# Evacuations of PE's results placed three blocks behind PE instead of one, in the expert part of a two-layer kernel

## The chip, the cores and the metric

The kernel runs on one core of a Trainium2 chip. The metric is the device time of one execution in microseconds. The kernel before took 1711.92 us, the median of three runs between 1710.94 and 1712.4 us. The execution that was profiled took 1712.86 us, of which the profile's span covers 1711.2 us.

## The reference, cut to what matters

Two transformer-like layers run one after the other on 256 tokens of width 1024, in float32. The change touches the last part alone, a mixture of 64 experts in 8 groups of 8. A router picks one group for each token and the two best experts in it:

```
def expert_block(args):
    xb, e = args
    hid = jax.nn.silu(xb @ w_gate[e]) * (xb @ w_up[e])
    return hid @ w_down[e]
```

`w_gate[e]` and `w_up[e]` are 1024 x 512 and `w_down[e]` is 512 x 1024, so each expert brings 6 MB of weights for the few tokens that chose it. The result of an expert is weighted by the token's gate and added to the residual, and a root-mean-square norm ends the computation.

## The kernel before, in words

**Tiling.** The tokens of a group are gathered into one tile. All 64 experts are computed on the tile of their group. Products are formed in a reduced float format from parts: a weight tile is split into a rounded part `whi` (a cast on ACT) and the rest `wlo` (a subtraction on DVE, which reads `whi`), by `split` at L107. For a *small* group (at most 64 tokens) the token tile holds the rounded part in columns 0 to 63 and the rest in 64 to 127, and two matmuls, one with `whi` and one with `wlo`, do the work. Seven of the eight groups are small; the group with the most tokens takes a full tile and three matmuls.

**Blocks.** The work is a list of blocks `order`, numbered s. An expert has four blocks for gate (here G1 to G4), four for up (G5 to G8), and four for down (D0, D1, R, D2). A down stage comes after the gate and up stages of the *next* expert. A G block is four matmuls of 128x512 in a small group, as are D0, D1 and D2. R is the down block that uses its weights unsplit (L1379), so it asks nothing of ACT and DVE. An expert thus asks for 11 splits of 128x1024. After D2 of one expert PE turns the hidden values of the next one (`pht`, L1284), which that expert's down stage needs. The split tiles come from pools of six `whi` and six `wlo` buffers. The raw weights lie in a ring of 11 tiles of 1 MB each (`ring`), six loads to an expert, issued from SP in order as the tiles come free.

**Order.** From block 9 on the instructions of PE, ACT and DVE stand in exactly the order in which the Python loop writes them. At each block s the loop writes the splits of block s + 3 (`AHEAD` is 3), then PE's matmuls of block s, then one step of every generator in `steps`, and then `follow(s)`, which starts new generators. Each engine takes its own instructions in that order, and one that waits holds up all behind it.

**The generators.** `copied` takes a gate or up sum out of PSUM to `gu` (on ACT for a small group, L1396). `turned` takes `pht` through Silu (`hs`, ACT, L1287), the product with up (`hs`, DVE, L1289), the rounded part (`hidThi`, ACT, L1292) and the rest (`hidThi`, DVE, L1294). `prepare` gathers the tokens of the next group (`oh` on DVE, `pgx` on PE at L1228, `xghi`), once in a group. `summed` ends a group: it splits the down sums (`yghi` on ACT, `yglo` on DVE), multiplies them back to token order (`psct`, PE) and adds them to the residual (DVE, L291). A step that reads a result of PE was written in the block right after the one in which PE's matmuls stand.

A *visit* is a run of experts of one group: three experts of group 0, then groups 1, 2, 3, 7, 4, 5 and 6 with eight experts each, then the last five of group 0. Group 7 is the one with the full tile. A load of an expert that no token chose is skipped while its matmuls are not.

Of the kernel before, what the change touches and what calls it, by code (L numbers as in the profile page):

```python
# [32 lines left out]
def mega(ctx, tc, a, out, dbg=None):  # L33
# [256 lines left out]
    def add_res(t, n, ps):  # L290
        nc.vector.tensor_tensor(xres[:, t, cols(n)], xres[:, t, cols(n)], ps, op=OP.add)  # L291


    ps = acc.tile([P, 4, P], F32, tag="acc", name="warm")
# [69 lines left out]
    ps = acc.tile([P, 512], F32, tag="acc", name="bps")  # L364
# [5 lines left out]
    for t in range(NT):  # L370
# [12 lines left out]
        for q in range(2):  # L383
            ps = acc.tile([P, 4, P], F32, tag="acc", name="sps")
            for i in range(4):
                g = 4 * q + i
                nc.tensor.matmul(ps[:, i, :], wsT[:, g, :], vs[:, t, g * P:(g + 1) * P], start=True, stop=True)
            for i in range(4):
                g = 4 * q + i
# [25 lines left out]
    done = set()  # L415
# [159 lines left out]
    for t in range(NT):  # L575
        for n in range(2):
            sl = slice(n * 512, (n + 1) * 512)
            ps = mm.tile([P, 512], F32, tag="mm", name="ppj")
            for k in range(2):
                mm3(ps, pTs, wpp[k], (al, k, ts(t)), (al, sl), k == 0, k == 1)  # L580
            x = nc.vector.tensor_copy(prj[:, t, sl], ps)
# [124 lines left out]
    ps = mm.tile([P, 512], F32, tag="mm", name="cps")  # L706
# [509 lines left out]
    def prepare(keys, b, small, xgs, gws, v):  # L1216

        oh = mq.tile([P, NT, P], F32, name="oh", bufs=1)
        for t in range(NT):
            nc.vector.tensor_scalar(oh[:, t, :], slot2 if small else slot, keys[t], None, op0=OP.is_equal)  # L1220
        yield
        xg = [x[:, b] for x in xgb]
        w = GS if small else P
        kn = 512 // w
        pss = [acc.tile([P, kn, w], F32, tag="acc", name="pgx") for _ in range(KD // kn)]
        for t in range(NT):
            for k in range(KD):
                x = nc.tensor.matmul(pss[k // kn][:, k % kn, :], tA[:, t, k, :], oh[:, t, :w],  # L1228
                                     start=t == 0 and k % kn == 0, stop=t == 1 and k % kn == kn - 1)
                if t + k == 0 and ranked:  # L1230
                    fence(x, ranked.pop())
        yield
        for q, ps in enumerate(pss):
            ks = slice(kn * q, kn * q + kn)
            halves(two(xg[0]), ps) if small else split_ps(xg[0][:, ks, :], xg[1][:, ks, :], ps)
        xgs[v] = xg
        yield
        pgw = mm.tile([P, 512], F32, tag="mm", name="pgw")
        for t in range(NT):
            nc.tensor.matmul(pgw[:, :8], oh[:, t, :], wsel[:, t, :], start=t == 0, stop=t == 1)  # L1240
        ps = acc.tile([P, 4, P], F32, tag="acc", name="poh")
        for t in range(NT):
            nc.tensor.transpose(ps[:, t, :], oh[:, t, :], ident)
        yield
        gw = mq.tile([P, 8], F32, name="gw")
        nc.vector.tensor_copy(gw, pgw[:, :8])
        ohT = mq.tile([P, NT, P], F32R, name="ohT")
        nc.scalar.copy(ohT, ps[:, :NT, :])
        gws[v] = gw, ohT
        yield  # L1250
# [26 lines left out]
    def turned(hids, i, pp, gw, small, plain, hl=None):  # L1277

        hl = hl or hl_tile(mp, [P, 4, P], "hidT")
        if small:  # L1280
            ps = mm.tile([P, 2, 4, GS], F32, tag="mm", name="pht")
            for j, x in enumerate(pp):
                for q in range(4):
                    nc.tensor.matmul(ps[:, j, q, :], x[:, ts(q)], pairs, start=True, stop=True)  # L1284
            yield
            h = mp.tile([P, 4, GS], F32, tag="wr", name="hs")
            nc.scalar.activation(h, ps[:, 0], AF.Silu)  # L1287
            yield
            nc.vector.tensor_tensor(h, h, ps[:, 1], op=OP.mult)  # L1289
            yield  # L1290
            n = 3 if plain else 4
            nc.scalar.copy(two(hl[0])[:, :n, 0], h[:, :n])  # L1292
            yield
            nc.vector.tensor_tensor(two(hl[0])[:, :n, 1], h[:, :n], two(hl[0])[:, :n, 0].bitcast(F32), op=OP.subtract)  # L1294
            hids[i] = h, hl
        else:
            ps = mm.tile([P, 4, P], F32, tag="mm", name="pht")
            for q in range(4):
                nc.tensor.transpose(ps[:, q, :], pp[0][:, ts(q)], ident)
            yield  # L1300
            last_copy[0] = nc.scalar.copy(hl[0], ps)
            yield
            nc.vector.tensor_tensor(hl[1], ps, hl[0].bitcast(F32), op=OP.subtract)
            hids[i] = None, hl
        yield
# [6 lines left out]
    def summed(pd, ohT, done=lambda *x: None):  # L1312

        yg = (gp.tile([P, D], F32R, tag="xn", name="yghi"), gp.tile([P, D], F32R, tag="xn", name="yglo"))
        for n in range(2):
            split_ps(yg[0][:, cols(n)], yg[1][:, cols(n)], pd[n])
            yield
        for n in range(2):
            for t in range(NT):
                ps = acc.tile([P, 512], F32, tag="acc", name="psct")  # L1320
                for i in range(2):
                    nc.tensor.matmul(ps, ohT[:, t, :], yg[i][:, cols(n)], start=i == 0, stop=i == 1)
                yield
                add_res(t, n, ps)
                done(t, n, ps)

    AHEAD = 3

    def moe(keys, expert, visits, small=lambda g: False, skip=False, begin=(), on_the_way=iter(())):
# [59 lines left out]
        def copied(i, kind):  # L1389

            v, g, e, es = todo[i]
            gw = gws[v][0][:, e:e + 1]
            ps = sums.pop((i, kind))
            if small(g):
                x = mq.tile([P, F], F32, tag="hid", name="gu")
                nc.scalar.copy(x, ps) if kind == "g" else nc.scalar.mul(x, ps, gw)  # L1396
                gus.setdefault(i, []).append(x)
            elif kind == "g":
                x = mq.tile([P, F], F32, tag="hid", name="hid")
                nc.scalar.activation(x, ps, AF.Silu)  # L1400
                gus[i] = [x]
            else:
                nc.vector.scalar_tensor_tensor(gus[i][0], ps, gw, gus[i][0], op0=OP.mult, op1=OP.mult)
            yield

        def follow(s):

            i, kind, c = order[s]
            v, g, e, es = todo[i]
            last = s + 1 == len(order) or order[s + 1][:2] != (i, kind)  # L1410
            if kind in "gu":
                if last:
                    steps.append(copied(i, kind))
                if kind == "u" and last and e == es[max(0, len(es) - 4)] and v + 1 < len(visits):
                    g2 = visits[v + 1][0]
                    steps.append(prepare(keys(g2), (v + 1) % 2, small(g2), xgs, gws, v + 1))
                if i == 0 and kind == "u" and last:
                    finish(steps)
                    steps.append(turned(hids, 0, gus.pop(0), gws[v][0], small(g), plain(0)))
                return  # L1420
            if i + 1 < n and (last if i + 2 < n else c == 1):
                g1 = todo[i + 1][1]
                hl = [x[:, (todo[i + 1][0] + 1) % 2, :4] for x in xgb] if i + 2 == n else None
                x = turned(hids, i + 1, gus.pop(i + 1), None, small(g1), plain(i + 1), hl)
                next(x)
                steps.append(x)
            if last and e == es[-1] and i < n - 1:
                steps.append(summed(pds.pop(v), gws[v][1]))

        def finish(gens):  # L1430
            for x in gens:
                for _ in x:
                    pass
            gens.clear()
# [9 lines left out]
        with ExitStack() as fixed:  # L1444
            for s in range(len(order)):
                while ahead < len(order) and ahead <= s + AHEAD:
                    fetch(ahead)
                    ahead += 1
                if s == 4:
                    after.clear()  # L1450
                multiply(s)
                if s == 0:
                    with soon():
                        finish([prep])
                        for f in begin[2:]:
                            f()
                if skip and s == 8:
                    fixed.enter_context(tc.manual_schedule(engines={
                        mybir.EngineType.PE, mybir.EngineType.Activation, mybir.EngineType.DVE}))
                if s > 120:  # L1460
                    next(on_the_way, None)
                for x in list(steps):
                    if next(x, steps) is steps:
                        steps.remove(x)
                follow(s)
            finish(steps)
        with soon():
            finish([summed(pds.pop(len(visits) - 1), gws[len(visits) - 1][1], squares)])


    for i in range(9):
# [79 lines left out]
```

## Time and profile before

| | us |
|---|---|
| median of three runs | 1711.92 |
| profiled execution | 1712.86 |
| its span | 1711.2 |
| PE matmul busy | 1650.8 (96%) |
| PE weight load busy | 1287.7 (75%) |
| DVE busy | 1352.2 (79%) |
| ACT busy | 1136.8 (66%) |

The expert part takes the span from about 690 us on. A busy PE row counts overlapping matmuls whose ends are modelled, so the weight loads (PEld), which come one for each matmul, show PE's pace better. Idle time stands in brackets behind the instruction that followed it, with the engine and line whose result ended it. Where the engine named had long been done, something else ended the wait.

### The profile page before, as it was taken

How to read it: one execution, taken by the hardware profiler on the slowest of the kernel's cores; microseconds unless marked ns; L12 is line 12 of the kernel's file. 1: busy time of each engine (PE TensorE's matmuls, PEld its weight loads, DVE VectorE, ACT ScalarE, POOL GpSimd, SP SyncE). 2: the span in 40 equal slices, each digit the busy share in tenths (PEclk: the TensorE clock that was granted, in tenths of full speed). 3: DMA queues.
4: the chain of work that ended last, by engine and by line, in shares of the span. 5: the costliest groups of instructions: out<-in, count | busy, mean ns of one | idle time of the engine just before them, and what ended most of it. 6: DMA issues, size and time to landing. Idle time of an engine off the chain costs nothing. (4 is left out here: it accounts for less than half of the span.)

```text
span 1711.2 us, 24078 instructions
## 1 busy us (share of the span) xinstructions
PE 1650.8 (96%) x8474; PEld 1287.7 (75%) x8474; DVE 1352.2 (79%) x1643; ACT 1136.8 (66%) x1542; POOL 44.6 (3%) x69
## 2 busy tenths in 40 slices
PE   8999999999999998999999999999999999999996
PEld 7898789998898787666667666788776666666664
DVE  6665675556768866898998898898998898898996
ACT  5455454445566544877777877776877877877884
POOL 1000010000100310000000000000000000000000
PEclk9999999999999997999999999999999999999998
DMA  9953455554743284996996999998999999999961
GB/s 316 260 173 124 164 176 197 188 181 158 201 148 101 109 313 163 402 398 244 374 395 243 404 398 377 407 373 332 369 386 385 407 398 381 416 398 378 412 248 38
DMA packets 124882, 493.52 MB, mean 288 GB/s; under 512 B 9150, under 2 KB 53538, under 8 KB 78161
## 3 DMA queue, kind: packets, MB, share of 16 engines
q1 hardware_dynamic: 120160, 484.47, 75.2%
q0 software_dynamic: 1952, 6.05, 1.2%
q10 hardware_dynamic: 2640, 1.38, 0.3%
q8 instruction: 68, 1.11, 0.3%
q14 instruction: 62, 0.50, 0.1%
HBM read 509.30 MB, written 1.44 MB: 298 GB/s over the span
## 5 line engine op out<-in xcount | busy, mean ns | idle before, releaser
L107 DVE TENSOR_TENSOR wlo<-ring,whi 128x1024 fp32r<-128x1024 f32 x714 | 836.6, 1221 | 106.3 <-ACT whi L107 105.4
L107 ACT CAST whi<-ring 128x1024 fp32r<-128x1024 f32 x714 | 704.5, 1048 | 15.2 <-PE pgu L1274 5.8
L1275 PE MATMUL pgu<-wlo,xghi 128*128 128x512 f32 x896 | 363.4, 406 | 11.1 <-DVE wlo L107 11.1
L1274 PE MATMUL pgu<-whi,xghi 128*128 128x512 f32 x896 | 357.1, 399 | 1.4 <-DVE xghi L1211 1.4
L107 DVE TENSOR_TENSOR wlo<-raw,whi 128x1024 fp32r<-128x1024 f32 x173 | 211.9, 1233 | 137.1 <-ACT whi L107 135.7
L107 ACT CAST whi<-raw 128x1024 fp32r<-128x1024 f32 x173 | 180.2, 1048 | 188.9 <-PE pb L115 81.0
L1275 PEld LDWEIGHTS pgu<-wlo,xghi 128*128 128x128 f32 x896 | 169.3, 189 | 78.7 <-DVE wlo L107 48.1
L1274 PEld LDWEIGHTS pgu<-whi,xghi 128*128 128x128 f32 x896 | 169.6, 189 | 31.8 <-DVE xghi L1211 1.6
L1275 PE MATMUL pd<-wlo,hidThi 128*128 128x512 f32 x332 | 142.1, 428 | 8.4 <-DVE wlo L107 8.4
L114 PE MATMUL pb<-hThi,whi 128*128 128x256 f32 x480 | 137.5, 286 | 0.2 <-ACT hThi L129 0.2
L1274 PE MATMUL pd<-whi,hidThi 128*128 128x512 f32 x332 | 136.8, 412 | 0.0
L115 PE MATMUL pb<-hTlo,whi 128*128 128x256 f32 x480 | 135.8, 283 | 0.5 <-DVE hTlo L130 0.5
L116 PE MATMUL pb<-hThi,wlo 128*128 128x256 f32 x480 | 135.8, 283 | 0.0
L1284 PEld LDWEIGHTS pht<-pairs,gu 128*128 128x128 f32 x896 | 108.2, 192 | 4.3
L1284 PE MATMUL pht<-pairs,gu 128*128 128x64 f32 x896 | 106.0, 271 | 0.0
L1275 PEld LDWEIGHTS pd<-wlo,hidThi 128*128 128x128 f32 x332 | 62.3, 188 | 57.0 <-DVE wlo L107 49.5
L1379 PE MATMUL pd<-ring,hs 128*64 128x512 f32 x216 | 104.2, 605 | 0.0
L1287 ACT ACTIVATE hs<-pht 128x256 f32<-128x256 f32 x56 | 21.5, 383 | 120.9 <-PE pht L1284 120.8
L1274 PEld LDWEIGHTS pd<-whi,hidThi 128*128 128x128 f32 x332 | 62.4, 188 | 51.4 <-ACT whi L107 43.0
L115 PEld LDWEIGHTS pb<-hTlo,whi 128*128 128x128 f32 x480 | 91.9, 191 | 1.4 <-DVE hTlo L130 0.7
L114 PEld LDWEIGHTS pb<-hThi,whi 128*128 128x128 f32 x480 | 91.9, 191 | 1.2 <-ACT hThi L129 0.5
L116 PEld LDWEIGHTS pb<-hThi,wlo 128*128 128x128 f32 x480 | 91.9, 191 | 0.0
(430 smaller groups left out, 2350.7 us busy)
## 6 DMA issues: line engine op xcount, KB each, us to landing
ring<-in_w_gate_dram SPq DMA_DIRECT2D x128, 1024.0 KB, 7.3
ring<-in_w_up_dram SPq DMA_DIRECT2D x128, 1024.0 KB, 7.2
ring<-in_w_down_dram SPq DMA_DIRECT2D x126, 1024.0 KB, 7.5
raw<-in_w_in_dram SPq DMA_DIRECT2D x38, 1024.0 KB, 5.3
raw<-in_w_ff_dram SPq DMA_DIRECT2D x32, 1024.0 KB, 5.1
raw<-in_w_out_dram SPq DMA_DIRECT2D x12, 1024.0 KB, 4.9
raw<-in_w_in_dram SPq DMA_DIRECT2D x9, 512.0 KB, 4.6
raw<-in_w_ple_gate_dram SPq DMA_DIRECT2D x4, 1024.0 KB, 5.1
```

Of the source, the lines that this page charges most:

```text
L107: both = [nc.scalar.copy(hi, raw), nc.vector.tensor_tensor(lo, raw, hi.bitcast(F32), op=OP.subtract)]
L114: nc.tensor.matmul(ps, l[0][lsel], r[0][rsel], start=first, stop=False)
L115: nc.tensor.matmul(ps, l[0][lsel], r[1][rsel], start=False, stop=False)
L116: nc.tensor.matmul(ps, l[1][lsel], r[0][rsel], start=False, stop=last)
L1274: nc.tensor.matmul(ps, x[0][:, k, :], w[0][wsel], start=first, stop=False)
L1275: nc.tensor.matmul(ps, x[0][:, k, :], w[1][wsel], start=False, stop=last)
L1284: nc.tensor.matmul(ps[:, j, q, :], x[:, ts(q)], pairs, start=True, stop=True)
L1287: nc.scalar.activation(h, ps[:, 0], AF.Silu)
L1379: nc.tensor.matmul(pds[v][m][:GS, :], h[:, 3, :], wt[:, 0, cols(m)], start=False, stop=False)
```

## The change

Every generator step that reads a result of PE is written three blocks behind PE's matmuls instead of one. A step now returns how many blocks to wait before the next one (nothing stands for one), and `steps` holds that count beside the generator. The residual additions of `summed` also come one `psct` later: the addition of one is written after the matmuls of the next. At the next-to-last expert all open generators are finished before its turn is started.

```
-        yield
+        yield AHEAD            # behind pgx, poh/pgw, both forms of pht
...
     def summed(pd, ohT, done=lambda *x: None):
+        wait = []
+        yield AHEAD - 1
...
-                yield
-                add_res(t, n, ps)
-                done(t, n, ps)
+                yield 2
+                if wait:
+                    wait.pop()()
+                wait.append(lambda t=t, n=n, ps=ps: (add_res(t, n, ps), done(t, n, ps)))
+        yield 2
+        wait.pop()()
...
         def copied(i, kind):
             v, g, e, es = todo[i]
+            yield AHEAD - 1
...
                 x = turned(hids, i + 1, gus.pop(i + 1), None, small(g1), plain(i + 1), hl)
-                next(x)
-                steps.append(x)
+                steps.append([next(x), x])
...
                 for x in list(steps):
-                    if next(x, steps) is steps:
-                        steps.remove(x)
+                    x[0] -= 1
+                    if x[0] == 0:
+                        r = next(x[1], steps)
+                        if r is steps:
+                            steps.remove(x)
+                        else:
+                            x[0] = r or 1
```

The first place is ACT around the Silu of one expert of a small group. `pht_7415` is the turned hidden values, and the six `whi` tiles with `ring_6035` to `ring_6037` belong to G1 to G6, the blocks that PE takes right behind `pht_7415`. Before:

```order
L1396 ACTIVATE gu_7384<-pgu_7347,gw_6260 128x512
L107 CAST whi_7390<-ring_6035 128x1024
L107 CAST whi_7398<-ring_6035 128x1024
L107 CAST whi_7405<-ring_6036 128x1024
L107 CAST whi_7424<-ring_6036 128x1024
L1287 ACTIVATE hs_7433<-pht_7415 128x256
L107 CAST whi_7436<-ring_6037 128x1024
L107 CAST whi_7445<-ring_6037 128x1024
L1292 CAST hidThi_7413<-hs_7433 128x3x64
```

The same place on ACT now:

```order
L107 CAST whi_7388<-ring_6035 128x1024
L107 CAST whi_7396<-ring_6035 128x1024
L1402 ACTIVATE gu_7402<-pgu_7345,gw_6260 128x512
L107 CAST whi_7405<-ring_6036 128x1024
L107 CAST whi_7424<-ring_6036 128x1024
L107 CAST whi_7434<-ring_6037 128x1024
L107 CAST whi_7442<-ring_6037 128x1024
L1287 ACTIVATE hs_7450<-pht_7415 128x256
L107 CAST whi_7453<-ring_6038 128x1024
L107 CAST whi_7462<-ring_6038 128x1024
L1292 CAST hidThi_7413<-hs_7450 128x3x64
```

The copy of the up sum, the Silu and the rounded hidden values each stand behind two more casts: the Silu behind the casts of G1 to G6 instead of G1 to G4.

The second place is DVE where a group of tokens ends. `yglo` is the rest of its down sums, `psct` the sums in token order, `xres` the residual. Before:

```order
L130 TENSOR_TENSOR yglo<-pd,yghi 128x512
L107 TENSOR_TENSOR wlo<-ring,whi 128x1024 x2
L1294 TENSOR_TENSOR hidThi<-hs,hidThi 128x3x64
L291 TENSOR_TENSOR xres<-xres,psct 128x512
L107 TENSOR_TENSOR wlo<-ring,whi 128x1024
L291 TENSOR_TENSOR xres<-xres,psct 128x512
L107 TENSOR_TENSOR wlo<-ring,whi 128x1024
L291 TENSOR_TENSOR xres<-xres,psct 128x512
```

The same place on DVE now:

```order
L130 TENSOR_TENSOR yglo<-pd,yghi 128x512
L107 TENSOR_TENSOR wlo<-ring,whi 128x1024 x2
L1294 TENSOR_TENSOR hidThi<-hs,hidThi 128x3x64
L107 TENSOR_TENSOR wlo<-ring,whi 128x1024 x2
L291 TENSOR_TENSOR xres<-xres,psct 128x512
L107 TENSOR_TENSOR wlo<-ring,whi 128x1024 x2
L291 TENSOR_TENSOR xres<-xres,psct 128x512
L107 TENSOR_TENSOR wlo<-ring,whi 128x1024 x2
```

The four additions are spread over eight blocks instead of four. The order of the loads on SP is the same in both kernels.

## Rows read from the trace of the kernel before

**Rows 1.** Page, part 1: busy us (share of the span) x instructions.

```profile
PE 1650.8 (96%) x8474; PEld 1287.7 (75%) x8474; DVE 1352.2 (79%) x1643; ACT 1136.8 (66%) x1542; POOL 44.6 (3%) x69
```

**Rows 2.** Waits, 700 to 1690 us: us in total, times, longest.

```profile
ACT hs L1287 <- PE pht L1284: 117.9, 53, 3.7
DVE wlo L107 <- ACT whi L107: 94.4, 117, 2.7
PEld pd L1275 <- DVE wlo L107: 47.7, 104, 1.0
PEld pgu L1275 <- DVE wlo L107: 46.9, 105, 0.9
PEld pd L1274 <- ACT whi L107: 42.2, 52, 0.8
...
PE pgu L1275 <- DVE wlo L107: 10.9, 49, 0.5
PE pd L1275 <- DVE wlo L107: 8.1, 15, 0.6
...
PEld pgx L1228 <- DVE oh L1220: 4.8, 6, 0.8
...
DVE wlo L107 <- DMA ring<-in_w_up_dram: 0.5, 2, 0.3
```

**Rows 3.** Weight loads, one ordinary expert: start us, us, instruction [idle before <-releaser].

```profile
1536.81 0.19 PEld L1275 LDWEIGHTS pgu<-wlo,xghi 128*128 128x128 f32 x1
1537.04 0.19 PEld L1274 LDWEIGHTS pgu<-whi,xghi 128*128 128x128 f32 x1
1537.50 0.19 PEld L1275 LDWEIGHTS pgu<-wlo,xghi 128*128 128x128 f32 x1 [0.27 <-DVE wlo L107]
1537.60 0.19 PEld L1274 LDWEIGHTS pgu<-whi,xghi 128*128 128x128 f32 x1
...
1538.90 0.19 PEld L1275 LDWEIGHTS pgu<-wlo,xghi 128*128 128x128 f32 x1 [0.64 <-DVE wlo L107]
...
1539.47 0.19 PEld L1274 LDWEIGHTS pd<-whi,hidThi 128*128 128x128 f32 x1
1540.04 0.19 PEld L1275 LDWEIGHTS pd<-wlo,hidThi 128*128 128x128 f32 x1 [0.37 <-DVE wlo L107]
...
1541.17 0.19 PEld L1275 LDWEIGHTS pd<-wlo,hidThi 128*128 128x128 f32 x1 [0.37 <-DVE wlo L107]
```

**Rows 4.** ACT, the same expert.

```profile
1531.93 0.38 ACT L1287 ACTIVATE hs<-pht 128x256 f32<-128x256 f32 x1 [2.06 <-PE pht L1284]
...
1546.88 0.38 ACT L1287 ACTIVATE hs<-pht 128x256 f32<-128x256 f32 x1 [2.07 <-PE pht L1284]
```

**Rows 5.** DVE, the same expert.

```profile
1533.29 1.22 DVE L107 TENSOR_TENSOR wlo<-ring,whi 128x1024 fp32r<-128x1024 f32 x1 [1.45 <-ACT whi L107]
...
1536.22 1.23 DVE L107 TENSOR_TENSOR wlo<-ring,whi 128x1024 fp32r<-128x1024 f32 x1 [0.24 <-ACT whi L107]
1537.36 0.35 DVE L1294 TENSOR_TENSOR hidThi<-hs,hidThi 128x192 fp32r<-128x192 f32 x1
```

**Rows 6.** ACT's Silu at the ends of a visit and of a gathering expert.

```profile
1499.48 0.38 ACT L1287 ACTIVATE hs<-pht 128x256 f32<-128x256 f32 x1 [2.06 <-PE pht L1284]
...
1516.98 0.38 ACT L1287 ACTIVATE hs<-pht 128x256 f32<-128x256 f32 x1 [3.72 <-PE pht L1284]
...
1566.61 0.38 ACT L1287 ACTIVATE hs<-pht 128x256 f32<-128x256 f32 x1 [1.36 <-PE pht L1284]
```

**Rows 7.** Groups by line, 700 to 1690 us: busy, mean ns | idle before.

```profile
L291 DVE TENSOR_TENSOR xres<-xres,psct 128x512 f32<-128x512 f32 x32 | 21.8, 683 | 0.0
L130 DVE TENSOR_TENSOR yglo<-pd,yghi 128x512 fp32r<-128x512 f32 x16 | 11.0, 688 | 7.4 <-ACT yghi L129 7.4
```

**Rows 8.** A window while the ring first fills; last columns: DMA share, GB/s.

```profile
635.00:640.00 5.00, 4.42 (x38) 4.12 (x38) 4.22 (x9) 3.22 (x7) 0.56 (x1) 1.00 1.02 424
```

**Rows 9.** Page, part 6: loads of gate weights, KB, median us from issue to landing.

```profile
ring<-in_w_gate_dram SPq DMA_DIRECT2D x128, 1024.0 KB, 7.3
```

More of the change, by code (lines that the diff above doesn't have):

```diff
@@ L1243, in prepare @@
             nc.tensor.transpose(ps[:, t, :], oh[:, t, :], ident)
-        yield
+        yield AHEAD
         gw = mq.tile([P, 8], F32, name="gw")
@@ L1284, in turned @@
                     nc.tensor.matmul(ps[:, j, q, :], x[:, ts(q)], pairs, start=True, stop=True)
-            yield
+            yield AHEAD
             h = mp.tile([P, 4, GS], F32, tag="wr", name="hs")
@@ L1299, in turned @@
                 nc.tensor.transpose(ps[:, q, :], pp[0][:, ts(q)], ident)
-            yield
+            yield AHEAD
             last_copy[0] = nc.scalar.copy(hl[0], ps)
@@ L1322, in summed @@
                     nc.tensor.matmul(ps, ohT[:, t, :], yg[i][:, cols(n)], start=i == 0, stop=i == 1)
-                yield
-                add_res(t, n, ps)
-                done(t, n, ps)
+                yield 2
[4 more added lines that the diff above has]
+        wait.pop()()
     AHEAD = 3
@@ L1412, in follow @@
                 if last:
-                    steps.append(copied(i, kind))
+                    steps.append([1, copied(i, kind)])
                 if kind == "u" and last and e == es[max(0, len(es) - 4)] and v + 1 < len(visits):
                     g2 = visits[v + 1][0]
-                    steps.append(prepare(keys(g2), (v + 1) % 2, small(g2), xgs, gws, v + 1))
+                    steps.append([1, prepare(keys(g2), (v + 1) % 2, small(g2), xgs, gws, v + 1)])
                 if i == 0 and kind == "u" and last:
                     finish(steps)
-                    steps.append(turned(hids, 0, gus.pop(0), gws[v][0], small(g), plain(0)))
+                    steps.append([1, turned(hids, 0, gus.pop(0), gws[v][0], small(g), plain(0))])
                 return
@@ L1422, in follow @@
                 g1 = todo[i + 1][1]
-                hl = [x[:, (todo[i + 1][0] + 1) % 2, :4] for x in xgb] if i + 2 == n else None
+                hl = None
+                if i + 2 == n:
+                    finish(steps)
+                    hl = [x[:, (todo[i + 1][0] + 1) % 2, :4] for x in xgb]
                 x = turned(hids, i + 1, gus.pop(i + 1), None, small(g1), plain(i + 1), hl)
-                next(x)
-                steps.append(x)
+                steps.append([next(x), x])
             if last and e == es[-1] and i < n - 1:
-                steps.append(summed(pds.pop(v), gws[v][1]))
+                steps.append([1, summed(pds.pop(v), gws[v][1])])
         def finish(gens):
-            for x in gens:
+            for _, x in gens:
                 for _ in x:
@@ L1453, in moe @@
                     with soon():
-                        finish([prep])
+                        finish([[0, prep]])
                         for f in begin[2:]:
@@ L1467, in moe @@
         with soon():
-            finish([summed(pds.pop(len(visits) - 1), gws[len(visits) - 1][1], squares)])
+            finish([[0, summed(pds.pop(len(visits) - 1), gws[len(visits) - 1][1], squares)]])
     for i in range(9):
```

## The prediction

> **What bounds the kernel now.** I read the page's busy times first, then the list of waits over the expert part, then one ordinary expert in order of time on PE, ACT and DVE, and last the loads.
>
> The busy times name PE as nearly full, with 96%, but its weight loads are busy for only 75% of the span, and DVE and ACT for 79% and 66% [rows 1]. So nothing says yet that an engine is at its limit. The list of waits shows a circle. ACT's Silu waits for PE's `pht` 53 times, 117.9 us in all; DVE's splits wait for ACT's casts, 94.4 us; and PE's weight loads wait for DVE's `wlo` 209 times, 47.7 + 46.9 = 94.6 us [rows 2]. DVE waits for a load of weights for 0.5 us only [rows 2], so the data lie ready.
>
> The reader can see the circle in one expert. Silu starts come every 14.95 us (1531.93 to 1546.88). Before each, ACT stands idle for 2.06 us, because the Silu needs `pht` and the casts of G5 and G6 stand behind it [rows 4]. DVE has then nothing to subtract from, idles 1.45 us until G5's cast is done, and 0.24 us more later [rows 5]. It now runs behind PE, and PE pays at four loads, with 0.27, 0.64, 0.37 and 0.37 us idle [rows 3].
>
> What do these cost PE? An undisturbed load follows the one before by 0.23 us (1536.81, 1537.04). The waiting one came 0.46 us after its forerunner and the next only 0.10 us after it: 0.56 us for a pair that takes 0.46 [rows 3]. So of an idle time about 0.17 us is not lost. The four cost 1.65 - 4 x 0.17 = about 1.0 us, and PE alone would need 14.95 - 1.0 = 13.95 us for an ordinary expert. DVE alone would need 14.95 - 1.45 - 0.24 = 13.26 us [rows 4, 5]. Over the whole stretch PE loses 94.6 - 209 x 0.17 = 59 us. This is the most that the change can give, with 6 x (0.8 - 0.17) = 4 us for `pgx` behind `oh` [rows 2]: 63 us.
>
> The waits of 42.2 us in 52 pieces for `whi` at `pd` I don't count. Mean and longest are both 0.8 us [rows 2]; a wait for a varying supplier isn't that even. They come right behind the unsplit products of R, and I take them for PE's own time. If I am wrong there, up to 52 x 0.64 = 33 us more could come back.
>
> **A reading of the page that would give another sum.** PE's own matmul row shows idle time of only 10.9 + 8.1 us before `wlo` [rows 2]; by that row the change can give about 19 us, and the time would be 1694. The Trainium skill (Perfetto Trace Analysis, Identifying the Most-Contended Engine) says that the busy share of matmuls is no good measure, since pipelined instructions overlap, and that the busy share of the weight loads is to be used. The loads' 94.6 us are what I use, for the reason shown at the pair of loads.
>
> **The change, part by part.** It adds no instruction and takes none away; the order of the loads on SP stays.
>
> *Ordinary experts.* In the order of ACT the Silu now stands behind the casts of G1 to G6, no longer G1 to G4. ACT had 2.06 us of idle time there [rows 4], room for two casts, and DVE can split G5 and G6 while it would have waited. So when PE starts on G1, DVE has up to two splits of 1.22 us [rows 5] less before it: 2.4 us, where PE's loss shows that 1.0 was lacking. The lead need not be won in one expert; DVE needs 13.26 us for what takes PE 13.95, so it gains 0.7 us in each. The six buffers bound it: the cast of G6 takes the buffer that the last down block D2 gives back, and D2 stands before `pht`, so ACT can have that cast done while `pht` runs. What is late next is PE itself. With 53 Silus of small groups, 8 group ends (32 additions, four each) and 6 gathering experts [rows 2, 7], some 39 experts are ordinary: 39 x 1.0 = 39 us.
>
> *Queues that the steps are moved past.* The copy of the up sum to `gu`, which `pht` needs, stands behind two more casts on ACT. PE takes the four down blocks in between (about a third of the expert, over 4 us), two casts and a copy on ACT are under 3 us, so I cost it at nothing as long as the weights lie ready; if they don't, PE waits for a load two blocks earlier than before. The rest of the hidden values (`hidThi` on DVE) stands behind two more splits: that is a rival below. No DMA is issued by a moved step, and SP waits for the same releases in the same order.
>
> *Gathering experts.* Their period is 1566.61 - 1546.88 = 19.73 us [rows 4, 6]. The four waits of an ordinary expert go (1.0) and that for `oh` (0.6), which stands behind the same splits of DVE: 6 x 1.6 = 10 us. The new place of `xghi` behind `pgx` hides under the three blocks that now lie between.
>
> *Group ends.* Their period is 1516.98 - 1499.48 = 17.5 us [rows 6]. What is left of the 59 us belongs here and to the edges of the full-tile group: 59 - 39 - 6 = 14 us. Here DVE has four additions of 0.68 us and two `yglo` of 0.69 more than usual, 4.1 us [rows 7], PE eight matmuls of 0.23, 1.8 us. DVE then needs 17.4 us for what takes PE 15.8, 1.6 us too many. Its lead covers about 1. Bounds: all 14 us come back, or none. I take 14 - 8 x 0.6 = 9 us.
>
> *The end.* At the last expert the Silu, the product and the parts are written together, and the last additions one after the other; between nothing and 3 us more, I take 1.
>
> Sum: 39 + 10 + 9 - 1 = 57 us off the profiled execution's 1712.86: 1656. The median of the runs shown lies 0.9 us below that execution, so 1655.
>
> **Rivals.**
>
> *The loads become the bound.* Six loads of 1 MB are 6.29 MB for an expert; in 14.95 us that is 421 GB/s. While the ring first fills, with no consumer, the loads come at 424 GB/s [rows 8], so an expert in 13.95 us asks for 451, which was never seen. The Trainium skill (HBM Reference, Specifications (TRN2)) gives about 425 GB/s for a core that streams alone, bounded by its 16 DMA engines; by that page an ordinary expert would take an estimated 14.8 us and the gain there would nearly vanish. The trace's 424 agrees with the page. Against the rival stands that the loads are ahead: a tile of the ring is used ten tiles after the load is issued, 10 x 14.95 / 6 = 24.9 us, and the load lands after 7.3 [rows 9]: 17.6 us of lead. At 424 GB/s an expert's loads take 14.84 us, 118.7 for a visit of eight; PE would take 6 x 13.95 + (17.5 - 1.1) + (19.73 - 1.6) = 118.2. A visit so costs 0.5 us of the lead, and three visits in a row don't use it up. If nevertheless the loads hold every ordinary expert at 14.95, only gathering experts and group ends gain, 10 + 9 us, and perhaps the lead of 17.6 once: 1675 to 1693, middle 1684.
>
> *Half of the lead is lost.* The six buffers, or ACT's own work between casts, could let DVE come only one split further instead of two, or the next wait take over, as the product `hs` on DVE for which ACT's rounded part waits. Then about half of the 57 us comes back: 1683.
>
> *No lead at all.* If the buffers already held ACT at G4 before, the moved Silu changes nothing: 1712. Against it speaks that the cast of G5 came right behind the Silu and not at a release by PE.
>
> *Slower: the hidden values come too late.* The rest `hidThi` on DVE stood behind the split of G7 and now stands behind that of D0. Before it ended at 1537.36 + 0.35 = 1537.71, 1.76 us before PE's first load of D0 at 1539.47 [rows 3, 5]. Two more splits are 2.44 us. If DVE gets no earlier in time, it is 0.7 us late at D0 in each expert, on top of the waits of now: 53 x 0.7 = 37 us, 1749. The point that decides is whether DVE is at least 0.7 us earlier than before when it takes up G5. The idle 1.45 us before G5 [rows 5] speaks against it.
>
> **How the numbers follow.** My forecast holds 0.74, with 1646 to 1667 as its own range: all 63 us and a few of the waits at `whi`, or 46. The loads as the bound have 0.11, half of the lead 0.08, no lead 0.03, slower 0.03; 0.01 is for more than all the waits. The range of 8 in 10 takes in the forecast and most of the first two rivals: 1645 to 1686. About 0.2% (3.4 us) is what a measurement of this kernel tells from no change. Faster: 0.94; the same: 0.03; slower: 0.03.
>
> **What would show it.** Right: ordinary experts with Silus 13.9 to 14.1 us apart, PE's waits for `wlo` from 94.6 to under 25 us, DVE's wait for `whi` under 50, and periods near 16.4 at group ends and 18.1 at gathering experts. If ordinary experts stay at 14.9 and DVE's or ACT's waits name the ring, the loads are the bound. If PE's loads wait for `hidThi` at D0, the last rival is at work. If the matmuls' cadence of 0.23 us itself changes, or waits for `whi` at `pd` shrink, my floor for PE was wrong.

## The result, and the profile after

| | before | after |
|---|---|---|
| median | 1712.16 us (1710.94 to 1715.5, four runs) | 1650.59 us (1646.12 to 1652.82, four runs) |
| profiled execution, its span | 1712.86, 1711.2 us | 1649.3, 1647.6 us |

The ratio is 0.9634, with an interval of 0.9609 to 0.966: 61.6 us less between the medians, 63.6 between the profiled executions. 57 were forecast, with 63 as the most that could come. Medians and ratios in this document are of executions at a mean granted clock of 0.93 or more; one of the four of five splits ahead (below) ran at 0.552, took 2673.68 us and is left out of its figures.

The page's busy times after, each with its share of the span and its instructions, answer to [rows 1]:

```profile
PE 1607.0 (98%) x8474; PEld 1303.9 (79%) x8474; DVE 1353.2 (82%) x1643; ACT 1147.2 (70%) x1542; POOL 44.7 (3%) x69
```

The instructions are as many as before, and DVE is busy for as long as before, ACT for 10 us longer. What went is idle time. PE's matmul row counts 44 us less than before for the same 8474 matmuls, so part of what that row counted as busy was waiting. The waits of the expert part after (who waited for what: us in all, times, longest) answer to [rows 2]:

```profile
DVE wlo L107 <- ACT whi L107: 50.2, 111, 1.5
...
PEld pd L1274 <- ACT whi L107: 34.9, 43, 0.8
ACT hs L1287 <- PE pht L1284: 33.1, 50, 0.9
...
PEld pgu L1275 <- DVE wlo L107: 3.5, 6, 0.9
PEld pd L1384 <- DMA ring<-in_w_gate_dram: 3.3, 9, 0.4
PEld psct L1324 <- DVE xres L291: 3.2, 4, 0.8
PEld psct L1324 <- DVE wlo L107: 2.4, 3, 0.8
...
ACT whi L107 <- DMA ring<-in_w_down_dram: 1.0, 3, 0.3
ACT whi L107 <- DMA ring<-in_w_gate_dram: 0.9, 3, 0.3
```

The circle has come apart in the order in which it was closed: the Silu's wait for `pht` from 117.9 us to 33.1, DVE's for the casts from 94.4 to 50.2, and the weight loads' for `wlo` from 94.6 to 5.9. Of these only the 3.5 at gate and up are waits for `wlo`: the 2.4 at `psct` belong to the row of `pd` for `whi`, which still has 0.8 us a piece. In both kernels 53 loads of this stretch come right behind R, and each of them has 0.81 us of idle time before it. Before, all 53 were loads of `pd`. Now 46 are, three of them put down to `gu`, and seven are loads of `psct`, put down to `xres` or `wlo`.

One ordinary expert shows it in order of time. First ACT (start, duration, engine, line, operation; in brackets the idle time before it and what ended it), as in [rows 4]:

```profile
1540.29 0.38 ACT L1287 ACTIVATE hs<-pht 128x256 f32<-128x256 f32 x1 [0.57 <-PE pht L1284]
1541.04 2.00 ACT L107 CAST whi<-ring 128x1024 fp32r<-128x1024 f32 x2 [0.36 <-PE pgu L1274]
...
1554.22 0.38 ACT L1287 ACTIVATE hs<-pht 128x256 f32<-128x256 f32 x1 [0.56 <-PE pht L1284]
```

The Silus are 13.93 us apart (before 14.95), and ACT stands idle before one for 0.57 us instead of 2.06. Behind the Silu its next cast waits 0.36 us for a matmul of G1, whose buffers it takes over. Then DVE in the same expert, as in [rows 5]:

```profile
1542.12 1.23 DVE L107 TENSOR_TENSOR wlo<-ring,whi 128x1024 fp32r<-128x1024 f32 x1 [0.43 <-ACT whi L107]
...
1546.19 0.35 DVE L1294 TENSOR_TENSOR hidThi<-hs,hidThi 128x192 fp32r<-128x192 f32 x1
```

And PE's weight loads there, as in [rows 3]:

```profile
1546.31 0.19 PEld L1274 LDWEIGHTS pgu<-whi,xghi 128*128 128x128 f32 x1
1546.53 0.19 PEld L1275 LDWEIGHTS pgu<-wlo,xghi 128*128 128x128 f32 x1
...
1547.21 0.19 PEld L1274 LDWEIGHTS pd<-whi,hidThi 128*128 128x128 f32 x1
...
1551.26 0.19 PEld L1274 LDWEIGHTS pd<-whi,hidThi 128*128 128x128 f32 x1 [0.81 <-ACT whi L107]
```

No load waits for `wlo`; the cadence is 0.23 us, as before. The rest of the hidden values ends at 1546.54 on DVE, and D0's first load starts at 1547.21: 0.67 us to spare, where it was 1.76. In the expert part PE's matmuls waited for `hidThi` once, 0.8 us at 831 us. The Silus of a group end and of a gathering expert answer to [rows 6]:

```profile
1450.59 0.38 ACT L1287 ACTIVATE hs<-pht 128x256 f32<-128x256 f32 x1 [0.46 <-PE pht L1284]
1466.44 0.38 ACT L1287 ACTIVATE hs<-pht 128x256 f32<-128x256 f32 x1 [0.92 <-PE pht L1284]
...
1494.31 0.38 ACT L1287 ACTIVATE hs<-pht 128x256 f32<-128x256 f32 x1 [0.57 <-PE pht L1284]
1511.76 0.39 ACT L1287 ACTIVATE hs<-pht 128x256 f32<-128x256 f32 x1 [0.91 <-PE pht L1284]
1526.36 0.38 ACT L1287 ACTIVATE hs<-pht 128x256 f32<-128x256 f32 x1 [0.92 <-PE pht L1284]
```

A group end takes 15.85 us (before 17.5), a gathering expert 17.45 (before 19.73). The expert after a gathering one takes 14.60, not 13.93, since PE's work on `poh` and `pgw` has moved past the next `pht`. So the two together are to be compared: 32.05 us against 19.73 + 14.95 = 34.68.

Last the loads, in one window (busy time of PE, PEld, DVE, ACT, POOL, then granted clock, DMA share, GB/s), and the row of the gate loads in the list of issues, the answer to [rows 9]:

```profile
1300.00:1350.00 50.00, 50.00 (x232) 36.96 (x231) 48.67 (x50) 43.27 (x55) 0.00 (x0) 1.00 1.01 421
```

```profile
ring<-in_w_gate_dram SPq DMA_DIRECT2D x128, 1024.0 KB, 10.0
```

From 1300 to 1550 us the loads run at 420 to 421 GB/s without a pause, close to the 424 of [rows 8]; over the whole kernel the gate loads land 10.0 us after their issue instead of 7.3. Yet ACT's casts waited for the ring in seven places only, 2.2 us in all, 1.9 of them in the last two rows of the waits above. So the loads are close behind PE; which of the two is the bound is tried below.

### The profile page after: what moved, and what is told of

Same layout as the page of the kernel before. It is cut to its first block, busy times and chain, and to the rows that moved or that the text cites. A ratio compares the mean times of both kernels' runs of the same rounds, so it can differ in the third digit from the quotient of the medians.

```text
span 1647.6 us, 24371 instructions
## 1 busy us (share of the span) xinstructions
PE 1607.0 (98%) x8474; PEld 1303.9 (79%) x8474; DVE 1353.2 (82%) x1643; ACT 1147.2 (70%) x1542; POOL 44.7 (3%) x69
## 5 line engine op out<-in xcount | busy, mean ns | idle before, releaser
L107 ACT CAST whi<-ring 128x1024 fp32r<-128x1024 f32 x714 | 712.4, 1048 | 74.0 <-PE pgu L1274 21.1
L1275 PE MATMUL pgu<-wlo,xghi 128*128 128x512 f32 x896 | 352.9, 394 | 1.1 <-DVE wlo L107 1.1
L1275 PE MATMUL pd<-wlo,hidThi 128*128 128x512 f32 x332 | 130.9, 394 | 0.0
L114 PE MATMUL pa<-whi,hThi 128*128 128x512 f32 x216 | 87.3, 407 | 3.3 <-ACT whi L107 1.7
L116 PE MATMUL pa<-whi,hTlo 128*128 128x512 f32 x216 | 85.5, 398 | 1.2 <-DVE hTlo L130 1.2
```

What stands on the lines that cost most here:

```text
L107: both = [nc.scalar.copy(hi, raw), nc.vector.tensor_tensor(lo, raw, hi.bitcast(F32), op=OP.subtract)]
L114: nc.tensor.matmul(ps, l[0][lsel], r[0][rsel], start=first, stop=False)
L116: nc.tensor.matmul(ps, l[1][lsel], r[0][rsel], start=False, stop=last)
L1275: nc.tensor.matmul(ps, x[0][:, k, :], w[1][wsel], start=False, stop=last)
```

## The experiments

Each ratio is to the kernel before, timed beside the run on the same chip. Those whose edit starts from the changed kernel say so.

### The turn alone, and all but the turn

The changed kernel, once with everything but `turned` back at one block, once with `turned` alone back:

```
# e1_turned_only: twice in prepare; summed as in the kernel before
-        yield AHEAD
+        yield
...
# and in copied
-            yield AHEAD - 1
...
# e2_all_but_turned: in turned, and where it is started
-            yield AHEAD
+            yield
...
-                steps.append([next(x), x])
+                steps.append([next(x) or 1, x])
```

> Only the reading of the turned hidden values (Silu, product, parts) stands three blocks behind PE; the copies of the gate and up sums, the gathering and the group ends stand one block behind, as before. Theory (ACT's halt at the Silu held back the splits of G5 and G6): ordinary experts 13.9 to 14.1 us apart, ACT's wait for the turned values from 118 to under 40 us; group ends and gathering experts gain less, about 1 us each lost of 14, so 1655 to 1668. Rival (each step behind PE holds ACT up for its share, the copies too): about half of the gain, near 1680 to 1690, with ordinary experts at 14.4.

> The counterpart: copies, gathering and group ends three blocks behind, the turned values one block behind as before. Theory: ordinary experts stay at 14.9 to 15.0 us and ACT still waits some 2 us at each Silu; only group ends and gathering experts gain, 5 to 15 us in all: 1697 to 1707. Rival (copies count): 1680 to 1690.

The turn alone took 1660.38 us (1658.7 to 1663.45), ratio 0.9691 (0.9675 to 0.9708). All but the turn took 1708.37 us, ratio 0.9967 (0.9954 to 0.9979), 1.4 us above the expected range. Away from group ends and gathering, ordinary experts took 13.93 us in the first and 14.96 in the second:

```profile
1534.12 0.39 ACT L1287 ACTIVATE hs<-pht 128x256 f32<-128x256 f32 x1 [0.21 <-PE pht L1284]
1548.05 0.39 ACT L1287 ACTIVATE hs<-pht 128x256 f32<-128x256 f32 x1 [0.22 <-PE pht L1284]
```

```profile
1590.58 0.39 ACT L1287 ACTIVATE hs<-pht 128x256 f32<-128x256 f32 x1 [2.06 <-PE pht L1284]
1605.54 0.39 ACT L1287 ACTIVATE hs<-pht 128x256 f32<-128x256 f32 x1 [2.06 <-PE pht L1284]
```

The waits of the first over the expert part:

```profile
ACT xghi L1210 <- PE pgx L1228: 21.8, 6, 5.3
...
ACT hs L1287 <- PE pht L1284: 10.2, 40, 0.8
...
PEld pgu L1275 <- DVE wlo L107: 3.5, 6, 0.9
```

And of the second:

```profile
ACT hs L1287 <- PE pht L1284: 129.4, 54, 4.1
...
PEld pgu L1275 <- DVE wlo L107: 47.3, 94, 0.9
```

The place of the turn by itself gives some 54 us, by the medians of the same rounds, and takes away nearly all of PE's waits for `wlo`. The other moves give 6 us by themselves and about 10 beside the turn. With the turn alone, a group end and the experts before and behind it took 14.6 + 15.2 + 14.6 = 44.4 us, with all moves 13.93 + 15.85 + 13.93 = 43.7; a gathering expert with its successor took 32.5 us, with all moves 32.05. The two alone add up to 60 us; the 62 of both is no more than that within the ratios' intervals. The turn was moved as a whole, so the shares of its four steps on ACT and DVE stay open.

### Five splits ahead instead of a step that comes later

The kernel before, with `AHEAD = 5`: what reads PE's result stands one block behind PE as before, but five splits stand ahead of it. Then the same with two more empty blocks behind `oh`, the mask that PE needs for `pgx`:

```
# e3_splits_five_ahead
-    AHEAD = 3
+    AHEAD = 5
# e9_five_ahead_early_oh: that, and in prepare, behind the writing of oh
         yield
+        yield
+        yield
```

> The kernel before with one number changed: the splits are written five blocks ahead of the matmuls instead of three, all steps stay one block behind PE. On ACT and DVE a step then stands behind the same split as in the changed kernel. Theory (what counts is how many splits stand ahead of the step, not how far it stands from PE's matmuls): ordinary experts at 13.9 to 14.0, 1648 to 1662. Rival (a step needs the three blocks of distance to PE): above 1680.

> The kernel before with splits written five blocks ahead, as in e3, and in addition the gathering's products two blocks further behind the one-hot tile (oh) that they read. Theory for what e3 lacked (PE waits 2.3 us for oh, which now stands behind two more splits on DVE, and in half of these places the granted clock then falls to 0.50): without that wait the clock stays at 1.0, gathering experts take 18 to 18.6 us and the time is 1647 to 1658. Rival (steps one block behind PE cost e3 its 22 us at other places, in ACT's wait for the gathered sums): above 1665 with gathering experts still over 20 us.

The first took 1672.84 us (1671.46 to 1679.29), ratio 0.9774 (0.9746 to 0.9803), between the ranges of its theory and its rival. Ordinary experts took 13.93, as expected, and group ends 15.9, but gathering experts 20.2 or 20.3 in three places and 23.4 to 25.1 in the other three. PE's weight loads for `pgx` in two of the six:

```profile
1405.12 3.65 PEld L1228 LDWEIGHTS pgx<-oh,tA 128*128 128x128 f32 x32 [2.32 <-DVE oh L1220]
...
1524.82 4.42 PEld L1228 LDWEIGHTS pgx<-oh,tA 128*128 128x128 f32 x32 [2.31 <-DVE oh L1220]
```

`oh` stands behind two more splits of DVE as well, and here the order counts the other way round: PE waits for DVE. With two more blocks between `oh` and the products that read it the kernel took 1649.0 us (1647.99 to 1651.33), ratio 0.9625 (0.9609 to 0.9641): no wait for `oh`, group ends of 15.89, and gathering experts of 17.52 (18 to 18.6 were expected; the next expert takes 14.60, as in the changed kernel):

```profile
1376.78 0.38 ACT L1289 ACTIVATE hs<-pht 128x256 f32<-128x256 f32 x1 [0.56 <-PE pht L1286]
1394.30 0.39 ACT L1289 ACTIVATE hs<-pht 128x256 f32<-128x256 f32 x1 [1.20 <-PE pht L1286]
```

This equals the changed kernel within the noise. What the reader of PE's result needs is independent splits ahead of it on ACT and DVE; whether they are put before it or it is put behind them is all one here, as long as what PE itself reads (`oh`) doesn't fall back with it.

### Five and four buffers

The changed kernel, with one or two of the six pairs of `whi` and `wlo` held by a tile whose last reader is written near the end of the program:

```
# e5_five_held; e6_four_held with range(2)
+        held = [wp.tile([P, 2, 512], F32R, tag="w" + x, ...) for _ in range(1) for x in ("hi", "lo")]
...
+                if s == len(order) - 2:
+                    for x in held:
+                        nc.vector.tensor_copy(ssf[:, 0, 0:1], x[:, 0, 0:1].bitcast(F32))
```

> The changed kernel with one of the six pairs of split buffers held unused through the expert part. Theory (the lead is bounded by the six pairs): the cast of G6, behind which the Silu stands, now takes the buffer of G1, which PE gives back only 0.9 us after the turned values are done; the Silu is about 2 us later and the hidden values come 0.5 us too late for D0: ordinary experts about 14.5, 1668 to 1690. Rival (the buffers have slack): no change, 1648 to 1653.

> The changed kernel with one of the six pairs of split buffers held back to the end of the expert part (its last reader now stands behind the last down block). Theory (the lead is bounded by the pairs): the cast of G6, behind which the Silu stands, takes the buffer that PE gives back after G1, 0.9 us behind the turned values; the Silu comes about 2 us later and the hidden values 0.3 to 0.7 us too late for D0: ordinary experts 14.2 to 14.7, 1660 to 1685. Rival (the pairs have slack): 1646 to 1653.

> The same with two pairs held, four left. The cast of G6 waits for G2 and the Silu for both, so the hidden values come some 1.5 to 3 us too late for D0 in each of 53 experts. This is the slower rival of the prediction made true: with the same order and no earlier DVE, 1700 to 1790, with PE's first down load waiting for the hidden values. If the order alone helped, it would stay under 1680.

In the first form the last reader came out ahead of the expert part, at 621 us, so the pair was free again and the run is a repetition of the changed kernel: 1648.65 us, ratio 0.9619 (0.9597 to 0.9641). It says nothing on buffers. With five pairs: 1686.87 us, ratio 0.9855 (0.9839 to 0.9872), 2 us above the expected range, ordinary experts 14.47 (0.54 more). With four: 1752.85 us, ratio 1.0237 (1.022 to 1.0254), slower than before, ordinary experts 15.51. An ordinary expert with five, then with four:

```profile
1328.07 0.38 ACT L1287 ACTIVATE hs<-pht 128x256 f32<-128x256 f32 x1
1342.54 0.38 ACT L1287 ACTIVATE hs<-pht 128x256 f32<-128x256 f32 x1
```

```profile
1619.54 0.38 ACT L1287 ACTIVATE hs<-pht 128x256 f32<-128x256 f32 x1
1635.05 0.38 ACT L1287 ACTIVATE hs<-pht 128x256 f32<-128x256 f32 x1
```

The waits with five:

```profile
ACT whi L107 <- PE pgu L1274: 85.4, 59, 1.7
DVE wlo L107 <- ACT whi L107: 82.5, 124, 3.4
...
PE pd L1274 <- DVE hidThi L1294: 17.2, 39, 1.0
```

And with four:

```profile
DVE wlo L107 <- ACT whi L107: 120.6, 168, 4.2
...
ACT whi L107 <- PE pgu L1274: 85.5, 63, 1.7
ACT whi L107 <- PE pd L1274: 73.6, 51, 4.9
...
PE pd L1274 <- DVE hidThi L1294: 35.7, 44, 1.5
```

A cast that waits for a matmul of PE waits for the buffer which that matmul reads; with six pairs ACT waited for `pgu` 14.6 us in all. With one pair fewer the Silu, in its new place, stands behind a cast that has no buffer yet. PE's matmuls then waited for `hidThi` 39 times with five pairs and 44 times with four. A weight load of D0 with five:

```profile
1333.96 0.19 PEld L1274 LDWEIGHTS pd<-whi,hidThi 128*128 128x128 f32 x1 [0.71 <-ACT gu L1402]
```

The rest of `hidThi` ended at 1333.84 on DVE, 0.1 us after the copy to `gu` that the row names, so it came last. Of 0.71 us idle about 0.54 is lost, by the 0.17 of the prediction, and 0.54 is what the expert takes longer. This is the slower rival of the prediction, made true by taking buffers away. The change needs all six pairs for its full gain; with five 25 us of it are left.

### The ring and the loads

The changed kernel, with a ring of seven tiles instead of 11, and with the up loads left out:

```
# e7_ring_seven
-    for i in range(9):
+    for i in range(5):
# e8_no_up_loads
+                if kind == "u":
+                    r = raws[i, "g", c // 2]
```

> The changed kernel with a ring of 7 tiles of raw weights instead of 11. A tile is then used six tiles after its load is issued, 6 x 13.93 / 6 = 13.9 us, less 7.3 to landing: 6.6 us of lead instead of about 16. Theory (the loads are ahead and PE bounds): little is lost, 1650 to 1668. Rival (the loads already hold the experts): each loses what the smaller lead gives up and ordinary experts rise above 14.8: over 1675.

> The changed kernel without the loads of the up weights: the up product uses the gate weights' tile, so a third of the expert bytes is left out and up has other values. Theory (PE bounds, the loads cost nothing): within 3 us of the changed kernel, 1645 to 1653, ordinary experts at 13.93. Rival (the loads at 421 GB/s hold the end or parts of the visits): 10 us or more faster.

With seven tiles: 1655.54 us, ratio 0.9668 (0.9652 to 0.9684), 5 us more than with 11. Its Silus, from where the lead was first used up:

```profile
1304.78 0.38 ACT L1287 ACTIVATE hs<-pht 128x256 f32<-128x256 f32 x1 [0.58 <-PE pht L1284]
...
1318.95 0.38 ACT L1287 ACTIVATE hs<-pht 128x256 f32<-128x256 f32 x1
...
1333.76 0.37 ACT L1287 ACTIVATE hs<-pht 128x256 f32<-128x256 f32 x1
...
1348.68 0.38 ACT L1287 ACTIVATE hs<-pht 128x256 f32<-128x256 f32 x1
```

Up to 1304 an ordinary expert took 13.93 us, then 14.17, 14.81 and 14.92; casts now waited for the ring, 8.0 us for gate and 5.2 for up loads. 6.29 MB in 14.9 us are 422 GB/s. Without the up loads: 1648.76 us, ratio 0.9633 (0.9616 to 0.9651), with the periods of the changed kernel and a third of the traffic less:

```profile
1300.00:1350.00 50.00, 50.00 (x232) 36.94 (x231) 48.67 (x50) 43.27 (x55) 0.00 (x0) 1.00 0.84 295
```

So the loads cost the changed kernel nothing that can be measured, and the lead of 11 tiles is what hides them: PE is the bound.

## Why the prediction was right

**Ordinary experts.** 13.95 us forecast, 13.93 measured. 31 plain ones gave 31.5 us, the six behind gathering experts 6.1 at the same rate, and the first experts with the edges of the full-tile visit about 3: 40 to 41 us for a term of 39. That this is PE's own pace is shown from three sides: an order with the same lead (five ahead) gives 13.93, a third fewer bytes gives 13.93, and the cadence stayed at 0.23. The way to it, pairs of loads in [rows 3] with 0.17 us of each wait not lost, held.

**A wait that is none.** The 0.8 us for `whi` behind R were taken for PE's own time. They stand at 0.81 after, although ACT's cast ended 0.43 us before the load at the median instead of 0.05. Seven of the 53 now stand before loads of `psct`, which read no `whi`, and have the same 0.81. So the row's total fell from 42.2 to 34.9 by names alone. Waits for `whi` at `pd` that shrink were named as a sign of a wrong floor; this fall is none. Five ahead with early `oh` has them too (39.8 us in 49 pieces).

**Matmul row or weight loads.** The matmul row's idle time would have given 19 us; 62 came. The Trainium skill (Perfetto Trace Analysis, Identifying the Most-Contended Engine) calls the busy share of matmuls no good measure and names the achieved FLOPs and the busy share of the weight loads instead. This trace agrees as far as the matmul row goes: it counted 44 us as busy that went with the waits.

**Gathering experts.** 18.1 + 13.95 = 32.05 us forecast for one with its successor, 32.05 measured, though divided otherwise (17.45 and 14.60). Beyond the ordinary share of the successor this is 6 x 1.6 = 10 us, as the term says.

**Group ends: the term that was mis-sized.** 16.4 us forecast, 15.85 measured. PE's own extra is 15.85 - 13.93 = 1.92 us, close to its eight matmuls' 8 x 0.23 = 1.84, so nothing of DVE's 4.1 us is left. I had let the lead cover 1 us of the 1.6 that DVE needs too many; it covered all. Nor did all eight ends gain: the one at which the full-tile visit begins took 18.92 us before and 19.13 after. Seven gave 7 x 1.65 = 11.5 us where the term had 9.

**The end.** 1 us of loss forecast. From the last ordinary Silu to the end of the span it was 1711.2 - 1673.85 = 37.35 us, and is 1647.6 - 1611.88 = 35.7, but 37.0 in the repetition of the changed kernel (the first form of five pairs). So there was no loss, and a gain of 0.3 to 1.6 that isn't clear of the spread between executions. From Silu to Silu the 63.6 us between the profiled executions are 31.5 + 6.1 + 3.1 (ordinary experts and edges) + 9.7 + 11.5 + 1.6.

**The loads as the bound.** The rival's premise was right and its price nil. An expert of 13.93 us asks for 6.29 MB, 451 GB/s, and the loads ran at 421; the Trainium skill (HBM Reference, Specifications (TRN2)) with its 425 agrees with the trace. But the lead suffices, as the smaller ring (5 us worse, bound in the last visits) and the run without up loads show from both sides.

**The other rivals.** Half a lead and no lead didn't come: the wait for `pht` fell by 85 us, the turn alone gave 54. The slower one stood nearer than its chance told: 0.67 us were to spare at D0, and one buffer pair fewer would have used them up.

DVE's waits for `whi` ended at 50.2 where under 50 was named, which changes nothing: DVE isn't what ends last.

## What to carry to other kernels

On engines that take their work in a written order, count how much independent work stands ahead of the instruction that waits for another engine; where a chain of idle times runs in a circle (ACT for PE, DVE for ACT, PE for DVE), two more pieces of work ahead of that instruction can open it at no cost. Look at the buffers first, since each piece of lead needs one (six pairs gained 62 us, five 25, and four lost 41), and look at the opposite direction, what PE reads, which must not come later (`oh`). To size it, take the lane whose cadence is undisturbed, subtract what each wait doesn't lose, and check against the total of the waits.

## What was not expected of the hardware

With five splits ahead PE's weight loads stood still for 2.3 us before `pgx` in all six gathering experts, its matmuls for 1.9. In three of them the granted clock fell 0.9 to 2.8 us after PE had taken up work again, and stayed low for 6.8, 6.8 and 10.2 us. The windows of one that did (columns as above), from the restart at 1524.82 on:

```profile
1525.00:1530.00 5.00, 5.00 (x33) 4.53 (x34) 2.23 (x2) 0.78 (x3) 0.00 (x0) 0.76 1.01 423
1530.00:1535.00 5.00, 5.00 (x12) 2.17 (x11) 1.92 (x2) 1.39 (x3) 0.00 (x0) 0.56 0.79 300
1535.00:1540.00 5.00, 5.00 (x33) 4.50 (x33) 2.27 (x3) 3.31 (x5) 0.00 (x0) 1.00 0.99 416
```

And of one that didn't, from 1405.12 on:

```profile
1406.00:1411.00 5.00, 5.00 (x31) 3.53 (x31) 2.72 (x4) 1.53 (x2) 0.00 (x0) 1.00 1.02 421
```

From 1527.6 to 1534.4 the clock stood at 0.50, which is 1.2 of 2.4 GHz. The three gathering experts with such a stretch took 23.4, 23.5 and 25.1 us, the others 20.2 or 20.3: 3.2, 3.2 and 4.8 us more, close to half of the 6.8, 6.8 and 10.2. That the standstill brought the low clock on was not tried by itself. With `oh` early there is no standstill, and the granted clock stayed at 1.0 from 664 to 1636 us; but that kernel's order differs as well. With held buffers PE stood still for 2.2 us near 681 us; with four pairs the clock fell at 682.1, with five it stayed. Why some of these alike waits were followed by it and others weren't stays open.
